# The opening loads of a hybrid attention, Fourier and Hyena layer: x, the first adaLN block and the first weights ahead of the filter constants

## The chip, the cores and the metric

The kernel runs on one core of one Trainium2 chip. The metric is device microseconds of one execution, the median of several runs. Every time below is counted from the start of the profiled execution's span unless it is called a duration.

## The reference

One layer of a diffusion backbone over 384 tokens (128 of context, 256 latent, in a grid 64 wide) of width 2048. Everything is float32.

```python
def _modulated_proj(x, cvec, norm_g, w_ada, b_ada, w_in):
    ada = jax.nn.silu(cvec) @ w_ada + b_ada
    shift, scale, gate = jnp.split(ada, 3, axis=-1)
    h = _rmsnorm(x, norm_g) * (1.0 + scale[:, None, :]) + shift[:, None, :]
    return h @ w_in, gate
...
    proj, gate = _modulated_proj(y, c_ctx[None, :], norm_g[l], w_ada[l], b_ada[l], w_in[l])
    q, k, v = _qkv(proj, q_norm_g[l], k_norm_g[l])
    att = _context_attention(q, k, v)
    kf = _hyena_filter_fft(len_prompt, f_w1[l], f_b1[l], f_freq[l], f_w2[l], f_b2[l], f_w3[l])
    y = _branches_residual(y, proj, gate, att, conv_w[l], conv_b[l], kf, hy_bias[l], w_br[l], w_out[l])
```

The Hyena filters come from a small network of two sine layers over positions and a last matrix f_w3, times a decaying window. They are normalised by the sum of their absolute values and taken to the frequency domain:

```python
    h = jnp.sin(f_freq * (z @ f_w1 + f_b1))
    h = jnp.sin(f_freq * (h @ f_w2 + f_b2))
    h = (h @ f_w3).astype(jnp.float32).reshape(L, HYENA_ORDER, 2, HY_W)
    h = h * jnp.exp(-t[:, :, None, None] * deltas)
    h = h / (jnp.sum(jnp.abs(h), axis=0, keepdims=True) + EPS)
    ...
    return jnp.fft.rfft(k2, axis=0)
```

## The kernel before

**Main work.** Weights stream from HBM in tiles of 256 rows by 512 columns (512 KB, tile w). ScalarE rounds each to a high part wh, VectorE takes the rest as a low part wl, and TensorE forms three products (high by high, low by high, high by low). The first stage of the main flow is hc_part: four column blocks of the Hyena input, taken in groups of rows (GROUPS). Group 0 needs the modulated activations h of the first 256 channels, group 1 those of the next 256, groups 2 to 4 of 512 more each. A group has 4 or 8 weight tiles, and a tile is 24 matmuls 384 columns wide.

**The adaLN blocks.** h exists only when the adaLN maps of its channels are done. ADA lists five blocks: first column, width, and at which main step (a main step is half a weight tile) their loads begin and how densely they follow. Blocks 0 and 1 are 256 channels wide (4 MB of w_ada each), blocks 2 to 4 are 512 wide (8 MB each). Block 0 has 8 loads, each a tile of 512 KB issued as two transfers of 256 KB, through N_ADA = 4 buffers. From block 1 on a step takes two loads. When a block's sums are complete, ada copies them to a row (ada_row), transposes it, forms scale and shift (am, sm) and modulates xT into h_hi and h_lo. The event h0 is block 0 done.

**Other opening work.** x_norm takes x in six tiles of 512 KB: a square with a row sum, transposes into xT, and at the end the reciprocal norm rstd_b. filters computes the sine layers f1 and f2, splits f_w3 on GpSimd (split_w3: a cast and a subtraction for each half), then forms 12 filter products of two matmuls 512 columns wide, each multiplied by the window win on VectorE into hw, and later sums of absolute values (habs), reciprocals, row broadcasts and the transforms specE, specO, specC. Those transforms are needed by hyena, which waits for hc, filters and all adaLN blocks.

**Order.** The class Weave decides the program order of TensorE and of the SP queue by a planned time: each flow (filters, ada_flow, x_norm, hyena, ada_gate, main, with a priority number, low first) yields steps with a planned TensorE time, a latency, events to wait for, and for loads the planned DMA time and the number of buffers. LOAD is the planned time of a 512 KB transfer, PAIR that of a weight tile on TensorE, X_AT the planned arrivals of x. Up to h0 the order of ScalarE, VectorE and GpSimd is the program's as well; after it a scheduler sets theirs. SP issues in order: a load whose buffer is not free holds up all loads behind it.

The loads before stand in this order. SP issues mlp (inputs of the sine layers), six tiles of x, win, then block 0 with the waits of its four buffers, and in between, after the fifth load, the first 512 columns of blob (Fourier matrices). GpSimd issues fw3 (f_w3) in two transfers, ScalarE's queue issues first (small vectors and the identity). The first weight tile is loaded when block 0 is through.

Of the kernel before, what the change touches and what calls it, by code (L numbers as in the profile page):

```python
# [18 lines left out]
P = 128  # L19
# [83 lines left out]

ADA = ((0, 256, -KT, 0), (256, 256, 0.1, 0.5), (512, 512, 4, 0.7), (1024, 512, 14, 1), (1536, 512, 30, 1))
GROUPS = ((0, (0,)), (1, (1,)), (2, (2, 3)), (3, (4, 5)), (4, (6, 7)))

BLOB = (("fwde", 256), ("fwdo", 256), ("inve", 256), ("invo", 256), ("fnetl", 516), ("fnetc", 130), ("chan", 256))
# [20 lines left out]
class Weave:  # L130
# [7 lines left out]

    def __init__(self):
        self.t = 0.0  # L140
        self.dma = 16.7
        self.flows = []
        self.events = {}
        self.slots = {}
        self.steps = 0
# [59 lines left out]
MM3 = 0.65  # L205
MM2 = 0.44
TR = 0.11
LOAD = 1.6
X_AT = (6.9, 8.4, 9.8, 12.7, 14.2, 15.6)
PAIR = 3.92  # L210


@with_exitstack
def hybrid_block(ctx: ExitStack, tc: tile.TileContext, a: dict):
# [25 lines left out]
    def s6(shape, dt, name):  # L240
        return big.tile(shape, dt, tag="s6", name=name, bufs=N_BIG)
# [24 lines left out]

    first = const.tile([P, 139 + P], F32, name="first")
    mlp = s6([64, TOK + 192], F32, "mlp")
    nc.sync.dma_start(out=mlp, in_=a["mlp"])
    nc.scalar.dma_start(out=first, in_=a["first"])  # L270
    vec, ident = first[:, 0:139], first[:, 139:139 + P]
    zfeat, fw1, fw2 = mlp[0:33, 0:TOK], mlp[0:33, TOK:TOK + 64], mlp[0:64, TOK + 64:TOK + 192]
    nmat = sum(w for _, w in BLOB)
    blob = hyc.tile([P, nmat], F32, name="blob")
    fw3 = [s6([P, 1024], F32, "fw3") for _ in range(2)]
    for q in range(2):
        nc.gpsimd.dma_start(out=fw3[q], in_=a["f_w3"][:, 1024 * q:1024 * q + 1024])
    win = s6([P, NT, HW], F32, "win")
    mats = {}
    c0 = 0  # L280
    for n, w in BLOB:
# [80 lines left out]
    def x_norm():  # L362

        ss = work.tile([P, 2, NT], F32, tag="ss", name="x_ss", bufs=1)
        arrival = iter(X_AT)
        for t in range(NT):
            for q in range(2):
                yield step(8 * TR, at=next(arrival))
                xt = xps[t, q]
                junk = s6([P, 1024], F32, "xjunk")  # L370
                nc.scalar.activation(junk, xt, AF.Square, accum_out=ss[:, q, t:t + 1])
                for g2 in range(2):
                    pt = acc()
                    for k in range(4):
                        c0 = 512 * g2 + P * k
                        nc.tensor.transpose(out=pt[:, P * k:P * k + P], in_=xt[:, c0:c0 + P], identity=ident)  # L376
                    (nc.scalar.copy, nc.vector.tensor_copy)[g2](out=xT[2 * q + g2][:, :, P * t:P * t + P],
                                                                in_=pt.rearrange("p (k c) -> p k c", k=4))
        s1 = work.tile([P, NT], F32, tag="ss1", name="x_s1", bufs=1)
        r1 = work.tile([P, NT], F32, tag="ss2", name="x_r1", bufs=1)  # L380
        yield step(0.0, lat=2.3)
        nc.vector.tensor_tensor(out=s1, in0=ss[:, 0], in1=ss[:, 1], op=ALU.add)
        yield step(0.0, lat=0.2)
        yield from rsqrt(r1, s1, NT, 1.0 / D)
        yield step(0.7, lat=0.3)
        pt = acc()
        for t in range(NT):
            mm(pt[:, P * t:P * t + P], r1[:, t:t + 1].broadcast_to([P, P]), ident)
        nc.scalar.copy(out=rstd_b, in_=pt[:, 0:TOK])
        W.signal("x")  # L390
# [6 lines left out]
    def ada(b, c0, wd, pace, rate):  # L397
# [2 lines left out]
        pa = None  # L400

        def load(i):
            w = adap.tile([P, nk, 2, wd], F32, tag="ada", name="w_ada", bufs=N_ADA)
            rows = w_ada[P * nk * i:P * nk * i + P * nk, 0:2 * D].rearrange("(k p) (t c) -> p k t c", p=P, t=2)
            for k in range(nk):
                nc.sync.dma_start(out=w[:, k], in_=rows[:, k, :, c0:c0 + wd])
            return w

        n = 1 if b == 0 else 2
        for i in range(0, KT // nk, n):  # L410
            yield step(0.48 * n, dma=n * LOAD, tag="ada", bufs=N_ADA // n, pace=pace + rate * nk * i)
            ws = [load(i + k) for k in range(n)]
            pa = pa or acc()
            for k in range(n * nk):
                kt = nk * i + k
                for j in range(4):
                    mm(pa[32 * j:32 * j + 32, 0:hw], cond[:, kt, :],
                       ws[k // nk][:, k % nk, j // 2, hw * (j % 2):hw * (j % 2) + hw], kt == 0, kt == KT - 1)
            if b == 0 and i == 4:
                nc.sync.dma_start(out=blob[:, 0:N_FWD], in_=a["blob"][:, 0:N_FWD])  # L420
                split(blob[:, 0:N_FWD].rearrange("p (q c) -> p q c", q=4), fwd_hi, fwd_lo)
        if b == 0:
            ahead.append(weights(w_in, 0, OFF_HC))
            next(ahead[0])
        yield step(nh * TR, lat=0.6, after=("x",), wait=1.0)
        with tc.high_priority():
# [37 lines left out]

    ahead = []

    def weights(src, kp, c0):

        w = stage.tile([P, 2, 512], F32, tag="w", name="w", bufs=N_W)
        nc.sync.dma_start(out=w, in_=src[256 * kp:256 * kp + 256, c0:c0 + 512].rearrange("(k p) c -> p k c", p=P))  # L470
        wh = stage.tile([P, 2, 512], F32R, tag="hi", name="wh", bufs=N_HI)
        wl = stage.tile([P, 2, 512], F32R, tag="lo", name="wl", bufs=N_LO)
        nc.scalar.copy(out=wh, in_=w)  # L473
        yield
        nc.vector.tensor_tensor(out=wl, in0=w, in1=wh.bitcast(F32), op=ALU.subtract)  # L475
        yield wh, wl

    def products(src, c0, kps, n, product, evac, done=lambda kp: (), final=False):


        ps = None
        for kp in kps:
            last = kp == kps[-1]
            rounds = (((0, 0), (1, 0), (0, 1)),) if last and final else (((0, 0), (1, 0)), ((0, 1),))
            for r, parts in enumerate(rounds):
                pe = 2 * len(parts) * PAIR / (6 * n)
                for j in range(n):
                    if (r, j) == (0, 0):
                        yield step(pe, dma=LOAD, tag="w", bufs=N_W, prep=2.3, count=2 * pe / PAIR, after=done(kp),
                                   wait=2.0)  # L490
                        with tc.high_priority():
                            *_, w = ahead.pop() if ahead else weights(src, kp, c0)
                        ps = ps or [acc() for _ in range(n)]
                    else:
                        yield step(pe, tag="w", bufs=N_W, count=2 * pe / PAIR)
                    for k in range(2):
                        for px, pw in parts:
                            product(ps[j], j, 2 * kp + k, px, w[pw][:, k, :], kp == kps[0] and k == px == pw == 0,
                                    last and k == pw == 1)
                    if last and (r, j) >= (len(rounds) - 1, 0):  # L500
                        with tc.high_priority():
                            evac(j, ps[j])
# [34 lines left out]
    def filters():  # L537
# [15 lines left out]
        f2 = yield from sin_layer(p2, P, 10, "f2")  # L553
        f2s = split(f2, tmp("f2h", None, F32R)[:, 0:TOK], tmp("f2l", None, F32R)[:, 0:TOK])
        fw3s.append(split_w3(fw3[1]))
        hw = [s6([P, NT, HW], F32, f"hw{j}") for j in range(4)]
        for jj, t in ((0, 0), (0, 1), (0, 2), (2, 0), (2, 1), (2, 2)):
            for j in (jj, jj + 1):
                yield step(MM2, lat=0.3, at=17.2)
                ph = aux()  # L560
                ts_, cs_ = slice(P * t, P * t + P), slice(512 * (j % 2), 512 * (j % 2) + 512)
                for i, f in enumerate(f2s):
                    mm(ph, f[:, ts_], fw3s[j // 2][:, cs_], i == 0, i == 1)
                nc.vector.tensor_tensor(out=hw[j][:, t, :], in0=ph, in1=win[:, t, :], op=ALU.mult)
        for s, ts in ((CONTEXT, (0,)), (LATENT, (1, 2))):
            pz = aux()
            for t in ts:
                yield step(0.0, lat=1.0)
                ab = [tmp("habs") for _ in range(4)]
                for j in range(4):  # L570
                    nc.scalar.activation(ab[j], hw[j][:, t, :], AF.Abs)
                yield step(1.0, lat=2.2, after=("h0",), wait=4.0)
                for j in range(4):
                    mm(pz[32 * j:32 * j + 32, :], ones, ab[j], t == ts[0], t == ts[-1])
            r = tmp("hrec")
# [293 lines left out]
    def ada_flow():  # L869
        for b, (c0, wd, pace, rate) in enumerate(ADA):  # L870
            yield from ada(b, c0, wd, pace, rate)
            if b == 2:
                late_constants()
        close_pool()
        W.signal("ada")

# [162 lines left out]
            yield from tok_block(w_out, 512 * ob, m, ev_out, final=(ob == 3), done=done)  # L1039

    x_loads()
    nc.sync.dma_start(out=win, in_=a["win"])
    E = mybir.EngineType
    with tc.manual_schedule(engines={E.PE, E.SP}):
        with tc.manual_schedule(engines={E.Activation, E.DVE, E.Pool}):
# [36 lines left out]
```

## Time and profile before

| | us |
|---|---|
| median of 3 runs | 1313.8 |
| lowest and highest | 1312.83, 1315.71 |
| profiled execution, time | 1315.51 |
| profiled execution, span | 1313.7 |
| TensorE busy in the span | 1281.3 |
| VectorE, ScalarE, GpSimd busy | 716.1, 461.7, 186.3 |

TensorE carries a matmul for 98% of the span, at a mean granted clock of 0.992. Durations below are those of the profiled execution, which is 1.7 us over the median; a change in time is worked out on it and carried over to the median.

### The profile page before, as it was taken

Reading aid. Unit: us, or ns where it says so; the run is one execution under the profiler, and the core shown is the slowest. Engines: PE = TensorE matmul, PEld = TensorE weight load, DVE = VectorE, ACT = ScalarE, POOL = GpSimd, SP = SyncE. Lnnn points to the kernel's source line nnn. Section 1 sums busy time; section 2 is a strip of 40 time slices with the busy share of each in tenths; the row PEclk is TensorE's granted clock in tenths of the full one; section 3 lists DMA queues with packets and bytes.
Section 4 is the critical chain, followed back from the end, with each engine's and each line's share of the span. In section 5 each row is a group of like instructions: output and inputs, shape, how many; then the busy total and the mean of one; then the engine's idle time right before and its main releaser. Section 6 shows DMA issues by size and latency. Waiting matters only on the chain.

```text
span 1313.7 us, 16781 instructions
## 1 busy us (share of the span) xinstructions
PE 1281.3 (98%) x6554; PEld 1072.6 (82%) x6554; DVE 716.1 (55%) x1077; ACT 461.7 (35%) x722; POOL 186.3 (14%) x201
## 2 busy tenths in 40 slices
PE   7899999999999999999999999999999999999997
PEld 4667879878888988889888888888888888888886
DVE  6566638878454225552344776565647652354442
ACT  4424324421344245432544333323333333242221
POOL 2046300135010002210110110011001100110000
PEclk9889999999999999999999999999999999999999
DMA  8788774322374545554443665554665544464551
GB/s 284 246 297 288 261 264 131 111 81 82 100 160 130 144 133 111 131 120 136 106 120 84 202 191 176 169 178 145 191 189 167 178 140 129 142 195 135 158 151 65
DMA packets 111183, 210.94 MB, mean 161 GB/s; under 512 B 8192, under 2 KB 16768, under 8 KB 111104
## 3 DMA queue, kind: packets, MB, share of 16 engines
q1 hardware_dynamic: 107200, 198.98, 49.2%
q0 software_dynamic: 3760, 10.76, 4.9%
q8 instruction: 51, 0.84, 0.3%
q14 instruction: 28, 0.23, 0.1%
q10 hardware_dynamic: 144, 0.14, 0.0%
HBM read 205.65 MB, written 4.19 MB: 160 GB/s over the span
## 4 chain that ended last, share of the span: by engine, by line
PE 94%; DMA 3%; DVE 1%; ACT 1%; POOL 1%; issue 0%; SPq 0%; ACTq 0%
PE acc L253 86%; PE aux L253 6%; DMA w<-in_w_in 1%; DMA w_ada<-in_w_ada 1%; DMA x<-in_x_prompt 1%; PE aux L851 0%; PE aux L783 0%; PE aux L996 0%; POOL yim L678 0%; DVE wl L475 0%; PE acc L376 0%; ACT wh L473 0%; PE aux L663 0%; POOL yre L678 0%; DVE f_n L529 0%
## 5 line engine op out<-in xcount | busy, mean ns | idle before, releaser
L475 DVE TENSOR_TENSOR wl<-w,wh 128x1024 fp32r<-128x1024 f32 x272 | 343.1, 1262 | 413.1 <-PE acc L253 304.2
L473 ACT CAST wh<-w 128x1024 fp32r<-128x1024 f32 x272 | 286.4, 1053 | 679.0 <-PE acc L253 586.3
L253 PE MATMUL acc<-wh,h_hi 128*128 128x512 f32 x912 | 361.0, 396 | 0.6 <-ACT gateA L743 0.6
L253 PE MATMUL acc<-wh,h_lo 128*128 128x512 f32 x912 | 356.1, 390 | 0.0
L253 PE MATMUL acc<-wl,h_hi 128*128 128x512 f32 x912 | 239.9, 395 | 0.0
L253 PEld LDWEIGHTS acc<-wh,h_hi 128*128 128x128 f32 x912 | 171.3, 188 | 36.4 <-ACT gateA L743 1.1
L253 PEld LDWEIGHTS acc<-wh,h_lo 128*128 128x128 f32 x912 | 171.5, 188 | 35.0 <-issue 0.7
L253 PEld LDWEIGHTS acc<-wl,h_hi 128*128 128x128 f32 x912 | 168.6, 188 | 34.4 <-issue 1.4
L253 PE MATMUL acc<-h_hi,wh 128*128 128x384 f32 x448 | 155.2, 347 | 5.7 <-DVE hc L634 2.0
L253 PE MATMUL acc<-h_lo,wh 128*128 128x384 f32 x448 | 151.6, 338 | 0.0
L931 DVE SCALAR_TENSOR_TENSOR gate_part<-w_gate,cond,gate_part 128x512 f32<-128x512 f32 x120 | 90.1, 796 | 43.4 <-DMA w_gate<-in_w_ada 43.3
L253 PEld LDWEIGHTS acc<-h_hi,wh 128*128 128x128 f32 x448 | 85.1, 190 | 16.6 <-issue 7.8
L253 PE MATMUL acc<-h_hi,wl 128*128 128x384 f32 x448 | 90.2, 339 | 0.0
L253 PEld LDWEIGHTS acc<-h_lo,wh 128*128 128x128 f32 x448 | 85.1, 190 | 2.2 <-issue 0.7
L1018 POOL TENSOR_TENSOR merged<-merged,mt 128x512 f32<-128x512 f32 x21 | 34.8, 1679 | 361.7 <-DVE mt L1017 361.7
L253 PEld LDWEIGHTS acc<-h_hi,wl 128*128 128x128 f32 x448 | 78.4, 188 | 3.4 <-issue 2.7
L253 PE MATMUL acc<-wh,m_hi 128*128 128x512 f32 x192 | 75.0, 390 | 0.0
L253 PE MATMUL acc<-wh,m_lo 128*128 128x512 f32 x192 | 74.8, 390 | 0.0
L253 PE MATMUL acc<-wl,m_hi 128*128 128x512 f32 x192 | 49.9, 390 | 0.0
L253 PEld LDWEIGHTS acc<-wh,m_hi 128*128 128x128 f32 x192 | 36.0, 188 | 7.4
L253 PEld LDWEIGHTS acc<-wh,m_lo 128*128 128x128 f32 x192 | 36.1, 188 | 7.4
L253 PEld LDWEIGHTS acc<-wl,m_hi 128*128 128x128 f32 x192 | 35.9, 188 | 7.3
(257 smaller groups left out, 1301.1 us busy)
## 6 DMA issues: line engine op xcount, KB each, us to landing
w<-in_w_in SPq DMA_DIRECT2D x208, 512.0 KB, 3.7
w_ada<-in_w_ada SPq DMA_DIRECT2D x48, 512.0 KB, 5.3
w<-in_w_br SPq DMA_DIRECT2D x32, 512.0 KB, 4.2
w_gate<-in_w_ada SPq DMA_DIRECT2D x64, 256.0 KB, 4.1
w<-in_w_out SPq DMA_DIRECT2D x32, 512.0 KB, 4.1
w_ada<-in_w_ada SPq DMA_DIRECT2D x32, 256.0 KB, 5.8
x<-in_x_sample SPq DMA_DIRECT2D x4, 512.0 KB, 12.3
bm<-in_rpb POOLq DMA_DIRECT2D x32, 64.0 KB, 6.0
```

Source lines behind the costliest of these rows:

```text
L253: nc.tensor.matmul(out, lhsT, rhs, start=start, stop=stop)
L473: nc.scalar.copy(out=wh, in_=w)
L475: nc.vector.tensor_tensor(out=wl, in0=w, in1=wh.bitcast(F32), op=ALU.subtract)
L931: nc.vector.scalar_tensor_tensor(out=part[s], in0=w, scalar=cond[:, kt, s:s + 1], in1=before, op0=ALU.mult, op1=ALU.add)
L1018: (nc.vector if ob == 3 and bi == 2 else nc.gpsimd).tensor_tensor(out=m32[:, t, :], in0=m32[:, t, :], in1=x, op=ALU.add)
```

## The change

The opening loads get another order, and the filter products another place:

- SP starts with x. mlp moves to ScalarE's queue, behind first.
- Block 0 is loaded at once behind x: all eight loads are issued before any of its matmuls. Loads 4 to 7 get buffers of their own (from the pool s6) in place of a wait on the first four. The first weight tile w0 is loaded just ahead of block 0's last load.
- fw3 moves from GpSimd's queue to SP, behind block 0. win and the blob columns move to SP behind the first main steps (pace 2.2).
- The 12 filter products wait for h0 and 7 planned us more; the blob split follows them. The planned wait for h0 that stood ahead of the habs sums goes.
- xjunk is one tile in place of six allocations.
- Planner constants: LOAD 1.6 to 1.42, PAIR 3.92 to 4.15, earlier X_AT, block 2's loads at 0.6 in place of 0.7 steps, blocks 3 and 4 from step 13 and 27 in place of 14 and 30.

```diff
-ADA = ((0, 256, -KT, 0), (256, 256, 0.1, 0.5), (512, 512, 4, 0.7), (1024, 512, 14, 1), (1536, 512, 30, 1))
+ADA = ((0, 256, -KT, 0), (256, 256, 0.1, 0.5), (512, 512, 4, 0.6), (1024, 512, 13, 1), (1536, 512, 27, 1))
...
-        self.dma = 16.7
+        self.dma = 10.5
...
-LOAD = 1.6
-X_AT = (6.9, 8.4, 9.8, 12.7, 14.2, 15.6)
-PAIR = 3.92
+LOAD = 1.42
+X_AT = (5.0, 6.3, 7.6, 8.9, 10.2, 11.5)
+PAIR = 4.15
...
-    nc.sync.dma_start(out=mlp, in_=a["mlp"])
     nc.scalar.dma_start(out=first, in_=a["first"])
+    nc.scalar.dma_start(out=mlp, in_=a["mlp"])
...
-    for q in range(2):
-        nc.gpsimd.dma_start(out=fw3[q], in_=a["f_w3"][:, 1024 * q:1024 * q + 1024])
     win = s6([P, NT, HW], F32, "win")
+
+    def filter_constants(*which):
+        for n in which:
+            if n < 2:
+                nc.sync.dma_start(out=fw3[n], in_=a["f_w3"][:, 1024 * n:1024 * n + 1024])
+            elif n == 2:
+                nc.sync.dma_start(out=win, in_=a["win"])
+            else:
+                nc.sync.dma_start(out=blob[:, 0:N_FWD], in_=a["blob"][:, 0:N_FWD])
...
+        junk = s6([P, 1024], F32, "xjunk")
...
-                junk = s6([P, 1024], F32, "xjunk")
...
-            w = adap.tile([P, nk, 2, wd], F32, tag="ada", name="w_ada", bufs=N_ADA)
+            if b == 0 and i >= N_ADA:
+                w = s6([P, nk, 2, wd], F32, "w_ada")
+            else:
+                w = adap.tile([P, nk, 2, wd], F32, tag="ada", name="w_ada", bufs=N_ADA)
...
+        ready = []
+        if b == 0:
+            for i in range(KT // nk):
+                if i == KT // nk - 1:
+                    w0 = weight_load(w_in, 0, OFF_HC)
+                ready.append(load(i))
+            filter_constants(0, 1)
         for i in range(0, KT // nk, n):
-            yield step(0.48 * n, dma=n * LOAD, tag="ada", bufs=N_ADA // n, pace=pace + rate * nk * i)
-            ws = [load(i + k) for k in range(n)]
+            yield step(0.56 * n, dma=n * LOAD, tag="ada", bufs=N_ADA // n, pace=pace + rate * nk * i)
+            ws = [ready[i]] if ready else [load(i + k) for k in range(n)]
...
-            if b == 0 and i == 4:
-                nc.sync.dma_start(out=blob[:, 0:N_FWD], in_=a["blob"][:, 0:N_FWD])
-                split(blob[:, 0:N_FWD].rearrange("p (q c) -> p q c", q=4), fwd_hi, fwd_lo)
         if b == 0:
-            ahead.append(weights(w_in, 0, OFF_HC))
+            W.dma += 3 * LOAD
+            ahead.append(weights(w_in, 0, OFF_HC, w0))
...
         fw3s.append(split_w3(fw3[1]))
+        yield step(0.0, pace=2.2)
+        filter_constants(2, 3)
+        W.dma += 2 * LOAD
...
-                yield step(MM2, lat=0.3, at=17.2)
+                yield step(MM2, lat=0.3, after=("h0",), wait=7.0)
...
+        split(blob[:, 0:N_FWD].rearrange("p (q c) -> p q c", q=4), fwd_hi, fwd_lo)
...
-                yield step(1.0, lat=2.2, after=("h0",), wait=4.0)
+                yield step(1.0, lat=2.2)
...
     x_loads()
-    nc.sync.dma_start(out=win, in_=a["win"])
```

weight_load is the allocation and load of a weight tile, taken out of weights without other change; products takes w0 as the first tile and plans no load for it.

## Rows read from the trace of the kernel before

**Rows 1.** The page: busy time of each engine, share of the span, instructions.
```profile
PE 1281.3 (98%) x6554; PEld 1072.6 (82%) x6554; DVE 716.1 (55%) x1077; ACT 461.7 (35%) x722; POOL 186.3 (14%) x201
```

**Rows 2.** Stretches: length, each engine's busy time (instructions), granted clock, DMA share, GB/s.
```profile
8.00:18.00 10.00, 7.63 (x30) 6.18 (x31) 4.83 (x6) 5.52 (x10) 6.82 (x4) 1.00 1.03 411
...
23.50:27.00 3.50, 3.50 (x41) 2.00 (x41) 3.43 (x11) 1.25 (x3) 0.00 (x0) 1.00 0.27 77
...
52.00:66.00 14.00, 14.00 (x143) 11.41 (x141) 6.16 (x16) 7.60 (x17) 1.03 (x2) 1.00 0.57 174
66.00:76.00 10.00, 7.47 (x63) 4.82 (x64) 6.92 (x13) 5.14 (x11) 0.00 (x0) 1.00 1.00 353
```

**Rows 3.** Timeline of the SP queue up to 26 us: start, duration, issue.
```profile
1.37 1.04 SPq L357 DMA_DIRECT2D x<-in_x_prompt  x2
...
12.53 0.37 SPq L406 DMA_DIRECT2D w_ada<-in_w_ada  x1
...
17.64 0.37 SPq L406 DMA_DIRECT2D w_ada<-in_w_ada  x1
...
25.42 0.88 SPq L406 DMA_DIRECT2D w_ada<-in_w_ada  x2
```

**Rows 4.** GpSimd's DMA queue, 4.5 to 8 us: packets, MB, share of 16 engines.
```profile
q0 software_dynamic: 119, 0.45, 47.6%
```

**Rows 5.** Timeline of TensorE, 22 to 40.9 us: start, duration, instruction [idle before].
```profile
22.39 0.39 PE L253 MATMUL aux<-fw3hl,f2h 128*128 128x512 f32 x1
22.62 0.40 PE L253 MATMUL aux<-fw3hl,f2l 128*128 128x512 f32 x1
...
24.72 0.64 PE L253 MATMUL acc<-w_ada,cond 128*32 128x128 f32 x16
...
33.31 0.42 PE L253 MATMUL acc<-w_ada,cond 128*32 128x128 f32 x8 [0.25 <-DMA w_ada<-in_w_ada]
34.01 0.42 PE L253 MATMUL acc<-w_ada,cond 128*32 128x128 f32 x8 [0.27 <-DMA w_ada<-in_w_ada]
...
36.70 0.65 PE L253 MATMUL acc<-w_ada,cond 128*32 128x128 f32 x8 [0.71 <-DMA w_ada<-in_w_ada]
...
40.17 0.69 PE L253 MATMUL acc<-h_hi,wh 128*128 128x384 f32 x1 [1.93 <-ACT h_hi L453]
```

**Rows 6.** TensorE's granted clock in stretches of 1 us: busy, clock, DMA share, GB/s.
```profile
44.00:45.00 1.00, 1.00 (x28) 0.50 0.90 317
...
78.00:79.00 1.00, 1.00 (x13) 0.50 1.03 393
```

**Rows 7.** Timeline of TensorE at the end of group 0, 73 to 76 us.
```profile
73.05 0.64 PE L253 MATMUL acc<-w_ada,cond 128*32 128x256 f32 x8 [0.71 <-DMA w_ada<-in_w_ada]
75.50 0.45 PE L253 MATMUL acc<-h_hi,wh 128*128 128x384 f32 x1 [1.81 <-ACT wh L473]
```

**Rows 8.** Timeline of the SP queue at the end of group 0.
```profile
50.83 15.66 SPq L406 DMA_DIRECT2D w_ada<-in_w_ada  x10
66.61 0.39 SPq L470 DMA_DIRECT2D w<-in_w_in  x1
```

**Rows 9.** VectorE's filter products and ScalarE's last filter copies by source line.
```profile
L564 DVE TENSOR_TENSOR hw<-aux,win x12: 680/682/692, 22.7 to 32.0; 128x512 f32<-128x512 f32 x12
...
L611 ACT COPY specC<-aux x2: 578/584/589, 125.6 to 170.3; 128x512 f32<-128x512 f32 x2
```

**Rows 10.** Timeline of TensorE: the transposes of block 4's rows.
```profile
198.19 0.44 PE L431 MATMUL aux<-first,ada_row 128*128 128x128 f32 x2 [0.70 <-DVE ada_row L428]
```

**Rows 11.** Timeline of VectorE and GpSimd, 14 to 41 us.
```profile
14.70 0.36 DVE L528 TENSOR_SCALAR f_n<-f_a 128x384 f32<-128x384 f32 x1
14.87 2.40 POOL L547 TENSOR_TENSOR fw3hl<-fw,fw3hl 64x1024 fp32r<-64x1024 f32 x1
15.10 2.40 DVE L529 TENSOR_SCALAR f_n<-f_n 128x384 f32<-128x384 f32 x1
...
38.74 1.40 DVE L452 SCALAR_TENSOR_TENSOR xT<-xT,am,rstd_b 128x256 f32<-128x256 f32 x4
```

## What the change is predicted to do

> **What bounds the kernel now.** First the page: TensorE carries a matmul for 1281.3 us [rows 1], so only about 32 us of the span can be won without taking work from it. What counts as busy at the opening is partly filler, so the opening is read next, stage by stage. The DMA engines are full at 411 GB/s from 8 to 18 us, then move 77 GB/s from 23.5 to 27 [rows 2]. The SP queue says why: its loads of block 0 need buffers that TensorE has to free, and after the early ones no pair goes out until 25.42 [rows 3]. TensorE reaches the first block-0 matmuls only at 24.72, behind transposes and filter products [rows 5]. From there on block 0 arrives late: its matmuls wait on loads that land 0.70 us apart (33.31, 34.01), the last starts at 36.70, and the first main matmul at 40.17 [rows 5]. The chain through the opening is therefore loads, not TensorE. After 40.17 it is mostly TensorE, with one hole: from 52 to 66 us the DMA engines are at 0.57, from 66 to 76 at 1.00, and TensorE loses 2.53 us there [rows 2] (10.00 less 7.47), most of it for a weight tile whose issue at 66.61 stood behind ten w_ada transfers [rows 7, 8]. The granted clock is 0.50 (1.2 GHz) from 44 to 45 us, still in the fifth us of main work, and again from 78 to 79, behind the hole [rows 6].
>
> **The first loads.** The last tile of x lands at 17.64: that issue was released by it, and the five tiles behind the second land from 12.53 on, 1.28 us apart (17.64 less 12.53, over 4) [rows 3]. Two things leave the front of x. GpSimd's queue moved fw3, taking 47.6% of the engines between 4.5 and 8 us [rows 4]; its 1.05 MB at 411 GB/s [rows 2] are 2.55 us. SP's own start with x moves from 1.37 [rows 3] to the place of mlp, some 0.6 us. mlp is still loaded and I book nothing for its move to ScalarE's queue. So x is complete at 17.64 - 2.55 - 0.6 = 14.5. Behind it come 16 transfers of block 0 at 0.70 us [rows 5] and w0, twice the bytes, at 1.4: 12.6 us, hence 27.1 for the last one. Before, that matmul started at 36.70. **Gain: 9.6 us.** Bounds: with 353 GB/s [rows 2], 0.74 us for 262 KB, it is 9.6 - 18 x 0.04 = 8.9, and without the 0.6 it is 8.3; with 411 GB/s, 0.64 us, it is 10.7.
>
> The own buffers are what makes this possible: SP now issues all of block 0 without a wait on TensorE, and what is queued behind them (fw3, then block 1) inherits no stall. x_norm hides under it: rstd_b needs x at 14.5, six squares and copies on ScalarE, and a short chain on VectorE that no longer has 12 multiplications of 0.68 us in between [rows 9]; 12 us of loads cover it. With that cover gone it would delay h0 one for one. The single xjunk costs nothing, since its writers are all on ScalarE, in order.
>
> The way from the last block-0 matmul to the first main one, 3.47 us (36.70 to 40.17) [rows 5], has the same instructions. The clock at the start of the main work I take as before: at 0.50 for the first 5 us.
>
> **The filter products.** They are 12 times two matmuls, 0.23 us apart (22.39, 22.62) [rows 5]: 24 x 0.23 = 5.5 us. Before they ran while block 0 was awaited; now they stand in the main stage, where TensorE is the bound. **Cost: 5.5 us.** Lower bound 0, if they fall into holes that TensorE has anyway; upper bound 8.2, if VectorE's 12 multiplications at 0.68 [rows 9] paced them. I take 5.5, because the new order puts them between the quarters of the second and third weight tile, some 1.1 us apart, which VectorE can follow. win must land before the fourth can go on; it is two load steps behind w0 and fw3 in the queue, and lands, at these rates, about when the second tile begins.
>
> **The constants behind.** fw3, win and blob, together 2.1 MB, are 5.7 us at 0.70 us per 262 KB that move past h0. Group 0 has the room: fw3, block 1, three weight tiles, win and blob are 7.9 MB, 21 us at that rate, from 27.1 on, to 48; TensorE has four tiles of 4.15 by PAIR, the products and the slow clock (5 us at half speed, 2.5 lost), 24.6 us from 30.6 on, to 55. So it costs nothing there while that cover lasts, else up to 5.7. The filters' end moves later by the same order; their last copies are at 170.3 [rows 9], and hyena also waits for block 4, whose rows come at 198.19 [rows 10]: 28 us of cover.
>
> **GpSimd's splits.** A subtraction of split_w3 takes 2.40 us, and a VectorE instruction that began in it took 2.40 where its like took 0.36 [rows 11]: the two exclude each other. Before, that fell beside the loads of x. Now fw3 lands at about 28.4, and the subtraction after the cast can meet the modulation that makes h0: by the offsets of [rows 5, 11] the four steps of 1.40 us begin at 38.74 - 9.6 = 29.1. **Cost: 0 to 2 x 2.4 = 4.8; I take 1.2**, half of one, as the two instructions needed first may slip ahead. The Trainium skill (GPSIMD Engine Reference, Specifications) says that GpSimd shares its SBUF interfaces with VectorE, in contention with two-port modes and two-input instructions. It speaks against this change, and the trace agrees by that 2.40. By the rule at its worst the sum below would lose nearly all its gain; by the row's half it keeps it.
>
> **The end of group 0.** Following the new constants step by step, one adaLN group more and four row broadcasts come to stand between the fourth and fifth weight tile. They fill the hole that is 0.71 + 1.81 now [rows 7], and the tile's load is queued behind fewer bytes at a time. I take 2.0 us of gain. Bounds: all of 2.5 and the slow clock after it, some 3 us, so 5.5; or a loss of 6, see below. PAIR nearer to what tiles take changes the order further on; I book 0, and 2 us either way for the range.
>
> **Sum:** -9.6 + 5.5 + 1.2 - 2.0 = -4.9. On the profiled execution (1315.5, of which 1313.7 are the span) that gives 1310.6; on the median 1313.8 it gives 1308.9. Differences under 0.2%, 2.6 us, are not told from no change here.
>
> **Rivals.**
> - **The hole closes entirely**, with the slow clock behind it: -9.6 + 5.5 + 1.2 - 5.5 = -8.4, and with the loads at their better bound -9.5: 1304 to 1305. For it: half of the engines' time stands idle just before the hole [rows 2]. Against: block 2's loads are packed denser, 0.6 for 0.7.
> - **The hole grows** (slower than before). The fifth weight tile is issued only after the adaLN groups ahead of it have found buffers; with eight transfers ahead, 2.1 MB at 353 GB/s [rows 2], it waits 5.9 us, and the clock falls after it, 3 us. -9.6 + 5.5 + 1.2 + 5.9 + 3 = +6: 1320. It decides as soon as the hole is 3 us longer than now, for then nothing is left. For it: the same 2.1 MB more stand ahead of block 2 relative to the main work. Against: the main work, too, has 5.5 us more to do meanwhile.
> - **GpSimd holds up h0**: both subtractions meet VectorE's needed steps, 4.8 in place of 1.2: -1.3, 1312.5, no measurable change. For it: the times computed above overlap. Against: the second comes 3.4 us after the first, when h0 should be made.
> - **The loads are no sooner**: the DMA engines are full before as after, so block 0 gains only the idle stretch 23.5 to 27, 3.5 x (1 - 0.27) = 2.6 us. Then -2.6 + 5.5 + 1.2 - 2.0 = +2.1: 1316. Against: 2.1 MB really leave its front.
>
> **How the numbers follow.** Chances: the forecast 0.46, the hole closed 0.20, the hole grown 0.13, GpSimd 0.14, loads no sooner 0.07. The likeliest gives 1309, with 1305 to 1313 as its own range from the bounds of loads and products. The range 1301 to 1317 takes in all but the hole grown in full and a little beyond the best. Faster: 0.40 of the forecast, all of the hole closed, a little of GpSimd: 0.62. Same: 0.06 of the forecast, most of GpSimd, some of the last: 0.22. Slower: the hole grown and some of the last: 0.16.
>
> **What would show it.** x complete near 14.5 with landings about 1.28 us apart; block 0's last matmul near 27 and the first main one near 31; no stretch of idle DMA before 40 us; the products between the quarters of tiles two and three, with no wait on win above 1 us; VectorE steps of 2.4 us near 30 if GpSimd interferes; TensorE idle near the fifth tile at most 1 us. The prediction is wrong if main starts later than 33, if that hole is longer than 5 us, or if idle time appears after 200 us, where I expect none.

## The result and the profile after

The changed kernel takes 1321.28 us (median of 4, 1319.04 to 1323.11); the kernel before, beside it, 1313.42 (median of 4). The ratio is 1.0056, 95% interval [1.0036, 1.0076]: 7.9 us slower, where 1309 was forecast, and outside the range. The profiled execution is the quickest of the four: 1319.04, its span 1317.3, 3.6 us over the span of before.

TensorE is busy for nearly the time of before, now 1276.7 of a longer span. One line of the page, to set beside [rows 1]:

```profile
PE 1276.7 (97%) x6554; PEld 1072.5 (81%) x6554; DVE 721.6 (55%) x1077; ACT 462.7 (35%) x722; POOL 185.2 (14%) x199
```

So the loss is idle time, and the opening is read first. TensorE's timeline from 22 us, to set beside [rows 5] (last column: idle before, and its releaser):

```profile
23.84 1.65 PE L253 MATMUL acc<-first,x_r 128*128 128x128 f32 x6 [3.96 <-DVE x_r L350]
25.42 3.23 PE L253 MATMUL acc<-w_ada,cond 128*32 128x128 f32 x80
...
36.25 0.69 PE L253 MATMUL acc<-h_hi,wh 128*128 128x384 f32 x1 [6.84 <-ACT h_hi L469]
37.13 0.69 PE L253 MATMUL acc<-h_lo,wh 128*128 128x384 f32 x1 [0.19 <-DVE h_lo L471]
```

The loads came out as forecast, but by two errors that cancel. The last x tile, issued by 3.84, landed at 12.94, 1.6 us sooner than the 14.5 forecast. From there to block 0's last load (27.23, 27.1 forecast) it took 14.3 us and not 12.6: block 0's transfers landed 0.75 us apart in place of 0.70, and w0 took 2.27 in place of 1.4. Block 0's last 80 matmuls run in one piece without a wait on a load and end at 28.65, 8.7 us before the end of 37.35 in [rows 5]. They stand on TensorE behind the broadcast of the reciprocal norm, which waits 3.96 us for x_r (23.84); so the chain of x_norm was not hidden by the loads to its end. But the first main matmul starts at 36.25, only 3.9 us before its 40.17. The way between the two is 7.60 us in place of 2.82, and TensorE idles 6.84 us of it for h_hi. The prediction had itself called a start after 33 its failure. What stands in that gap is on three other engines. GpSimd from 20 us:

```profile
28.57 1.04 POOL L569 CAST fw3hl<-fw 128x1024 fp32r<-128x1024 f32 x1 [27.25 <-DMA fw<-in_f_w]
29.69 2.34 POOL L570 TENSOR_TENSOR fw3hl<-fw,fw3hl 64x1024 fp32r<-64x1024 f32 x1
32.09 1.04 POOL L569 CAST fw3hl<-fw 128x1024 fp32r<-128x1024 f32 x1
33.21 2.40 POOL L570 TENSOR_TENSOR fw3hl<-fw,fw3hl 64x1024 fp32r<-64x1024 f32 x1
```

VectorE and ScalarE in the same stretch:

```profile
29.59 0.22 DVE L457 TENSOR_TENSOR sm<-aux,first 128x2 f32<-128x2 f32 x2
29.72 2.39 DVE L459 TENSOR_TENSOR am<-am,first 128x2 f32<-128x2 f32 x2
32.17 4.25 DVE L468 SCALAR_TENSOR_TENSOR xT<-xT,am,rstd_b 128x256 f32<-128x256 f32 x4
```
```profile
25.91 1.05 ACT L493 CAST wh<-w 128x1024 fp32r<-128x1024 f32 x1
34.21 1.05 ACT L493 CAST wh<-w 128x1024 fp32r<-128x1024 f32 x1 [7.26 <-DMA w<-in_w_in]
35.17 1.83 ACT L469 ACTIVATE h_hi<-xT,sm 128x256 fp32r<-128x256 f32 x4
```

Two things meet. Two am steps, each two elements wide, take 2.39 us together where their like take 0.22, and four xT steps 4.25 where they take 1.40 [rows 11]: 5.0 us together. The am steps end with the first subtraction (32.11 and 32.03), the xT steps run through the second (33.21 to 35.61). And ScalarE holds, ahead of h_hi, the cast of the *second* weight tile, which waits 7.26 us for its load. Before, only the first tile's cast stood there. SP shows why that load is late: it is issued at 26.51, behind fw3 and the first four transfers of block 1.

```profile
20.49 1.09 SPq L281 DMA_DIRECT2D fw<-in_f_w  x2
22.06 4.06 SPq L417 DMA_DIRECT2D w_ada<-in_w_ada  x4
26.51 0.37 SPq L485 DMA_DIRECT2D w<-in_w_in  x1
```

Further on, TensorE is busy throughout the products (the first two of 24, which run from here to 59.6):

```profile
46.79 0.39 PE L253 MATMUL aux<-fw3hl,f2h 128*128 128x512 f32 x1
47.02 0.39 PE L253 MATMUL aux<-fw3hl,f2l 128*128 128x512 f32 x1
```

One starts 0.23 us behind the other: 24 x 0.23 = 5.5 us, as forecast (from start to next start, all 24 take 5.7). The hole at the end of group 0 is still there, now as three waits on block 2's loads in place of [rows 7], and later waits on other engines follow:

```profile
71.06 0.64 PE L253 MATMUL acc<-w_ada,cond 128*32 128x256 f32 x8 [0.69 <-DMA w_ada<-in_w_ada]
73.10 0.64 PE L253 MATMUL acc<-w_ada,cond 128*32 128x256 f32 x8 [0.40 <-DMA w_ada<-in_w_ada]
75.36 1.08 PE L253 MATMUL acc<-w_ada,cond 128*32 128x256 f32 x8 [1.62 <-DMA w_ada<-in_w_ada]
...
104.27 0.41 PE L253 MATMUL acc<-h_hi,wh 128*128 128x384 f32 x1 [1.16 <-DVE hc L661]
```

The stretches, to set beside [rows 2] (length; busy time and count of TensorE, weight load, VectorE, ScalarE, GpSimd; granted clock, DMA share, GB/s):

```profile
23.50:27.00 3.50, 3.16 (x38) 2.83 (x42) 0.25 (x2) 1.43 (x2) 0.00 (x0) 0.54 1.06 384
40.00:42.00 2.00, 2.00 (x11) 2.00 (x10) 0.01 (x1) 0.00 (x0) 0.00 (x0) 0.79 0.06 14
52.00:66.00 14.00, 14.00 (x140) 11.02 (x139) 9.41 (x23) 6.13 (x13) 0.00 (x0) 1.00 0.54 166
66.00:76.00 10.00, 7.08 (x64) 3.49 (x62) 6.12 (x10) 4.50 (x10) 0.00 (x0) 0.95 0.98 334
```

The early DMA idleness is gone (384 GB/s from 23.5 to 27, 77 before), but a new one stands at 40 to 42 us (14 GB/s, before 376), and the hole from 66 to 76 is 2.92 us, before 2.53. The load of the fifth weight tile is issued later than the 66.61 of [rows 8], behind twelve transfers of block 2 in place of ten:

```profile
45.93 23.27 SPq L417 DMA_DIRECT2D w_ada<-in_w_ada  x12
69.33 0.39 SPq L485 DMA_DIRECT2D w<-in_w_in  x1
```

### The profile page after: what moved, and what is told of

Same layout as the page of the kernel before. It is cut to its first block, busy times and chain, and to the rows that moved or that the text cites. A ratio compares the mean times of both kernels' runs of the same rounds, so it can differ in the third digit from the quotient of the medians.

```text
span 1317.3 us, 16793 instructions
## 1 busy us (share of the span) xinstructions
PE 1276.7 (97%) x6554; PEld 1072.5 (81%) x6554; DVE 721.6 (55%) x1077; ACT 462.7 (35%) x722; POOL 185.2 (14%) x199
## 4 chain that ended last, share of the span: by engine, by line
PE 90%; issue 3%; DMA 2%; DVE 2%; ACT 1%; POOL 1%; SPq 0%; ACTq 0%; POOLq 0%
PE acc L253 83%; PE aux L253 5%; DMA w<-in_w_in 1%; DMA mlp<-in_mlp 1%; DMA w_ada<-in_w_ada 0%; PE aux L810 0%; PE aux L1024 0%; DVE wl L495 0%; PE aux L878 0%; DVE xT L468 0%; POOL yim L705 0%; ACT wh L493 0%; DVE cm L704 0%; ACT xjunk L379 0%; PE acc L384 0%
## 5 line engine op out<-in xcount | busy, mean ns | idle before, releaser
L253 PE MATMUL acc<-h_hi,wl 128*128 128x384 f32 x448 | 93.5, 341 | 0.0
```

The source lines that it names most:

```text
L253: nc.tensor.matmul(out, lhsT, rhs, start=start, stop=stop)
```

## The experiments

Twelve kernels ran, each beside the kernel before. For the early stretch a mark is used below: the start of VectorE's rounding rest wl of the 25th weight tile, at 202.22 us before and 204.99 after, so +2.8. From there to the last tile the differences of the runs move by 0.9 to 2.5 us more. A mark is that of one execution, and the profiled executions lie between 2.2 us under their kernel's median (the changed kernel) and 2.9 over it (the second tile ahead); so a difference of marks of 3 us or less, without a wait that accounts for it, does not rank two kernels. The medians do.

**Splits out of the way.** In the changed kernel a one-column GpSimd copy of h_lo stands ahead of the splits:

```diff
+            guard = const.tile([P, 1], F32, name="guard")
+            nc.gpsimd.tensor_copy(out=guard, in_=hl[0][:, 1, 0:1].bitcast(F32))
+            fw3s.extend(split_w3(fw3[q]) for q in range(2))
```

> The changed kernel with GpSimd's two splits of fw3 held back until h0 is made: a one-column copy of the last part of h_lo stands ahead of them on GpSimd. Loads, and the order on TensorE, VectorE, ScalarE and SP, are those of the changed kernel. Theory (the two subtractions cost VectorE's modulation 5.0 us): the steps on the way to h0 take 0.22 and 1.40 us again, the first main matmul comes near 31.5 in place of 36.25, the products do not wait (their operand is split by 41), and the time is 4 to 5 us under the changed kernel, so 2 to 4 us over the kernel before. Rival (the head start is lost again before 200 us, since the loads of block 1 and the weight tiles, not TensorE, then set the pace): main starts as early, but the 25th weight tile comes less than 2 us earlier than in the changed kernel. Second rival (GpSimd's splits now meet the first low parts of the weights): the low parts of tiles one and two take 2.4 us more, and half of the gain goes.

Measured 1318.91, ratio 1.0039 [1.0021, 1.0058]. VectorE's chain is short again, but the first main matmul comes at 36.20 and not near 31.5, because ScalarE waits as before:

```profile
29.51 0.22 DVE L466 TENSOR_TENSOR am<-am,first 128x2 f32<-128x2 f32 x2
29.78 1.41 DVE L475 SCALAR_TENSOR_TENSOR xT<-xT,am,rstd_b 128x256 f32<-128x256 f32 x4
```
```profile
34.41 1.04 ACT L503 CAST wh<-w 128x1024 fp32r<-128x1024 f32 x1 [7.40 <-DMA w<-in_w_in]
35.36 1.49 ACT L476 ACTIVATE h_hi<-xT,sm 128x256 fp32r<-128x256 f32 x4
```

The splits do stretch VectorE; alone they do not decide.

**Second tile's load ahead of fw3,** splits as changed:

```diff
+            loaded.append(weight_load(w_in, 0, OFF_HC + 512))
             filter_constants(0, 1)
```

> The changed kernel with one load moved: the second weight tile is loaded right behind block 0, ahead of fw3; the GpSimd splits stay where the change put them. Theory (two blockers in a row, VectorE held up by the GpSimd splits and ScalarE held up by the cast of the second weight tile, which waits for its load): that cast now runs near 29 us without a wait, fw3 lands some 1.4 us later, VectorE is still held up by the splits, so the first main matmul comes between 33.5 and 36.5 in place of 36.25, and the time is 0 to 2.5 us under the changed kernel, 1318.5 to 1321. Rival (the splits alone hold h0): the first main matmul at 36 to 38, 1320 to 1323. Rival (the second tile's cast alone): first main matmul near 31.5, 1316 to 1317.

Measured 1321.23, ratio 1.0058 [1.0042, 1.0074], no faster than the changed kernel. The cast now runs at 28.93. A first matmul slips in at 31.95, but then TensorE waits 5.30 us and goes on at 37.94: the rival (the splits alone hold h0) was right on time and place.

```profile
31.95 0.69 PE L253 MATMUL acc<-h_hi,wh 128*128 128x384 f32 x1 [2.60 <-ACT h_hi L470]
37.94 0.69 PE L253 MATMUL acc<-h_lo,wh 128*128 128x384 f32 x1 [5.30 <-DVE h_lo L472]
```
```profile
29.93 5.13 DVE L469 SCALAR_TENSOR_TENSOR xT<-xT,am,rstd_b 128x256 f32<-128x256 f32 x4
34.99 3.55 DVE L472 SCALAR_TENSOR_TENSOR h_lo<-xT,sm,h_hi 128x256 fp32r<-128x256 f32 x4
```

**Both together,** the two edits above:

> The changed kernel with both suspects removed: the second weight tile is loaded right behind block 0, ahead of fw3, and the GpSimd splits wait until h0's activations are made. Theory: h_hi starts near 30.5, the first main matmul comes at 31 to 32 in place of 36.25, and 4.5 to 5 us of it reach the end: 1316 to 1317, 1 to 3 us over the kernel before. Rival (a third cause stands behind the two): the first main matmul after 33.5. Rival (the early start is lost again in group 0 because block 1 or the later tiles are not there yet): main starts at 31 to 32 but the time stays at 1319 to 1321.

Measured 1315.11, ratio 1.0012 [0.9996, 1.0027]: 2.1 us over before, not told from no change, and 6.2 under the changed kernel. Main starts at 31.45, as the theory said, with ScalarE and VectorE without a stretched step:

```profile
28.54 1.04 ACT L504 CAST wh<-w 128x1024 fp32r<-128x1024 f32 x1 [1.80 <-DMA w<-in_w_in]
30.60 1.49 ACT L477 ACTIVATE h_hi<-xT,sm 128x256 fp32r<-128x256 f32 x4 [1.02 <-DVE xT L476]
```
```profile
31.45 0.69 PE L253 MATMUL acc<-h_hi,wh 128*128 128x384 f32 x1 [1.97 <-ACT h_hi L477]
```

So there were two blockers, either of which held h0 until 36. But of the 8.7 us by which main starts earlier than before, 5.5 go to the products, and the other 3.2 are gone at the 25th tile, which stands at +0.4. From the first main matmul to the mark TensorE idles 8.24 us, before 6.72; the longest waits are 1.52 us on w_ada at 71.25 and 2.06 on ada_row at 146.56. So 1.5 us are added idle time; the rest is matmuls that start further apart, some of them at a granted clock of 0.50 from 148 to 150 us, right behind the second wait. That rest was not taken apart.

**fw3 behind the first main steps.** filter_constants(0, 1) and both splits move behind `yield step(0.0, pace=2.2)`:

> The changed kernel, with the loads of fw3, and so GpSimd's two splits of it, moved from behind block 0 to behind the first main steps, ahead of win; nothing else. Theory (GpSimd's subtractions hold up VectorE's modulation that makes h0): in the changed kernel the steps L459 and L468 took 2.39 and 4.25 us where the kernel before has 0.22 and 1.40, 5.0 us together, so here they take 0.2 and 1.4 again, the first main matmul comes at 31 to 32 in place of 36.25, and the time falls by about 4.5 us against the changed kernel, to the level of the kernel before or 1 us under it. Rival (the way to h0 is slow for another reason, such as full DMA engines or the later x): first main matmul stays near 36, time within 1 us of the changed kernel. Second rival (the head start is won, but the weight and block-1 loads now 1 MB further back or the holes behind take it again): main starts near 31, time falls by less than 2 us.

Measured 1327.00, ratio 1.0098 [1.0077, 1.0119]: slower, though main starts 2.8 us earlier than in the changed kernel. The mark is at +10.2. VectorE shows where it went: reciprocals of the filter sums, which now come due beside block 1, stand ahead of its ada_row, and TensorE idles 5.84 us at 65.84.

```profile
60.83 3.39 DVE L603 RECIPROCAL hrec<-hrec 128x128 f32<-128x128 f32 x4
...
65.50 0.28 DVE L443 COPY ada_row<-acc 128x128 f32<-128x128 f32 x1
```

**The same, reciprocals behind h1** (`yield step(0.0, after=("h1",))` ahead of hrec):

> The kernel of e1_fw3_late (1327.0) with one planned wait more: the reciprocals of the filter sums wait for h1, the second adaLN block. Theory (in e1_fw3_late the head start of 2.8 us was lost where VectorE had four reciprocals, 3.4 us, and what they wait for ahead of block 1's row, so that TensorE idled 5.84 us before it, with a slow clock after): the idle time before block 1's row falls under 1.5 us, and the time by 6 to 10 us, to 1317 to 1321. Rival (the loss lay in fw3 and its splits coming late for the products): no change from 1327.

Measured 1315.95, ratio 1.0008 [0.9992, 1.0024], the mark at +1.5: 11 us better by that one wait. That settles where the run before it lost its time.

**fw3 early, as before the change,** on GpSimd's queue ahead of everything, the rest as changed:

> The changed kernel with fw3 loaded from GpSimd's queue at the start again, as in the kernel before; nothing else. Theory (GpSimd's subtractions are the loss): the splits fall at 10 to 18 us beside x, where they can slow the sine layer's VectorE steps but not h0; block 0 lands 2.5 us later, since 1 MB shares the engines with x again; the first main matmul comes at 33 to 34.5; time 2 to 3 us under the changed kernel, so 3 to 5 us over the kernel before. Rival (the two kernels differ by the position of fw3 on the DMA engines alone): main starts 2.5 us later than in the changed kernel, near 38.5, and the time rises by 2.5.

Measured 1320.17, ratio 1.0043 [1.0029, 1.0056]. VectorE's am and xT steps are 0.22 and 1.41 us again, yet main starts at 37.34, between theory and rival. fw3's bytes explain part: x is complete at 15.82, 2.9 us later than in the changed kernel. But rstd_b is copied at 30.68, 5.2 us later (25.53), because the splits, now at 10.42 to 17.70, hold the VectorE steps of the first sine layer instead:

```profile
11.78 2.41 DVE L553 TENSOR_SCALAR f_n<-f_n 64x384 f32<-64x384 f32 x1
14.23 3.88 DVE L555 SCALAR_TENSOR_TENSOR f_a<-f_n,f_a 64x384 f32<-64x384 f32 x2
```

In the changed kernel these take 0.35 and 1.14 us. TensorE waits 4.14 us for f_a, and the last transposes of x, block 0 and the norm's broadcast stand behind it. These 4.8 us beside x are as much as the splits cost beside h0 (5.0).

**Splits out of the way, and mlp first on SP,** to ask whether its landing at 8.34 us (3.62 before) matters:

> The kernel of e5_splits_wait_h0 with mlp at the head of SP's queue again in place of second on ScalarE's. Theory (in the changed kernel mlp landed at 8.4 us where it had landed at 3.7, because ScalarE's two loads share the engines with x; the sine layers and the transposes of x wait for it on TensorE, and rstd_b stands ahead of block 0's last five loads until 25.4): rstd_b comes 1 to 3 us earlier, x itself 0.4 later, h0 0.5 to 1 us earlier than in e5_splits_wait_h0, the time 0 to 1 us under it. Rival (block 0's loads alone set h0): no difference or 0.4 us more.

Measured 1320.28, ratio 1.0046 [1.0029, 1.0063]. mlp is used at 3.62, and rstd_b is copied at 22.68, 2.6 us earlier than in the run with the splits moved (25.31). But x is complete at 14.07 and block 0's last load lands at 28.90 (13.01 and 27.43 there), and the second tile's cast, held by its load until 35.90, still stands ahead of h_hi: main starts at 37.69. Nothing is gained while the loads and that cast set h0.

**The products alone moved,** on the kernel before:

```diff
-                yield step(MM2, lat=0.3, at=17.2)
+                yield step(MM2, lat=0.3, after=("h0",), wait=7.0)
...
-                yield step(1.0, lat=2.2, after=("h0",), wait=4.0)
+                yield step(1.0, lat=2.2)
```

> The kernel before with one part of the change alone: the 12 filter products, and their planned wait, behind h0. Theory (a product is TensorE time that was free before h0 and is paid in full behind it, 24 matmuls at 0.23 us): 5.5 us more behind h0, less what block 0 gains since its matmuls no longer stand behind five products, at most 2.7 us: slower than the kernel before by 3 to 5.5 us. Rival (they fill holes that TensorE has in the main stage anyway): same as the kernel before, or up to 2.6 us faster.

Measured 1339.28, ratio 1.0192 [1.0170, 1.0214]: far beyond both expectations. Block 0's matmuls end no sooner (38.45, before 37.35), and TensorE idles 9.35 us ahead of block 1's row at 77.10; on VectorE the four reciprocals (72.08, 3.39 us) stand ahead of ada_row (76.76). It is the jam of the run with fw3 late, found here in another kernel. The mark is at +21.6: beside the 9.35 and the products' 5.5 there is another wait of 4.70 at 122.10 (on VectorE's scaling of hw); the rest was not followed.

**The planner's constants alone,** on the kernel before (ADA, LOAD, PAIR):

> The kernel before with the planner's constants of the changed kernel alone: LOAD, PAIR, and the paces and starts of blocks 2 to 4. Theory (the constants only shift which instructions stand next to each other, and explain the rest of the loss: 1.2 us of holes before 200 us and 0.9 behind): slower than the kernel before by 1 to 3 us. Rival (they are what lengthened the hole at the end of group 0, and the rest is chance): slower by 3 us or more. Second rival: no difference.

Measured 1315.67, ratio 1.0009 [0.9997, 1.0022]: no difference told. The mark is at -2.9, the last tile at -1.9, but the profiled execution (1313.61) is the quickest of the twelve, so this is no gain. From the mark to the last tile 1.0 us is given back, and as much in the whole change (+2.8 to +3.7). This part comes with the constants: behind 205 us TensorE idles 5.35 us here and 5.30 in the changed kernel, before 4.61, and both have a wait of 0.7 us for ScalarE's pT (at 663.12 and 668.72) that the kernel before lacks. The constants also put the twelve transfers of block 2 ahead of the fifth weight tile, whose load is issued at 70.04 here.

**Block 0's loads alone,** own buffers and all issued at once, on the kernel before:

> The kernel before with the loads of block 0 alone changed: all eight issued at once behind x and win, four of them into buffers of their own, the first weight tile ahead of the last. fw3 stays at the start on GpSimd's queue, win behind x, the filter products stay before h0, and the constants are those of before. Theory (the loads are worth what the waits on buffers cost, and the loss lies in the products' move): x complete at 17.6 as before, win 1.9 us more, 12.6 us of loads: the last block-0 matmul at 32 in place of 36.7, the first main one at 35.5 to 36.5, the time 3 to 5 us under the kernel before. Rival (block 0's matmuls stand behind transposes, products and rstd_b on TensorE, so earlier loads help little): main starts at 38 or later, time within 2.6 us of the kernel before.

Measured 1315.02, ratio 1.0013 [0.9999, 1.0027]. Main starts at 40.58. What was won on the loads is held on ScalarE by what stands ahead of h_hi: blob's cast and the habs behind it, then both weight tiles' casts.

```profile
34.48 0.62 ACT L301 CAST fwd_hi<-blob 128x512 fp32r<-128x512 f32 x1 [1.76 <-DMA blob<-in_blob]
35.00 2.19 ACT L584 ACTIVATE habs<-hw 128x512 f32<-128x512 f32 x4
37.10 1.03 ACT L486 CAST wh<-w 128x1024 fp32r<-128x1024 f32 x1
38.78 1.04 ACT L486 CAST wh<-w 128x1024 fp32r<-128x1024 f32 x1 [0.66 <-DMA w<-in_w_in]
39.73 1.49 ACT L462 ACTIVATE h_hi<-xT,sm 128x256 fp32r<-128x256 f32 x4
```

**The same with the second tile's load behind block 0 and blob ahead of it** (blob is loaded behind win, and the broadcast of the norm gets a planned time of 27 us; the three edits were not told apart):

> The kernel before with block 0's loads all issued at once (buffers of their own), the first and the second weight tile and blob around them, the filter products left where they were. Theory (in this version what held h0 was ScalarE's queue, with casts of blob and of the second weight tile that waited for loads ahead of h_hi): the first main matmul at 38 to 39 in place of 40.17, 1 to 2 us under the kernel before, 1312 to 1313.5. Rival (fw3 and win ahead of x and the products on TensorE hold block 0 itself, so nothing is won): first main matmul at 40 or later, 1314 to 1316.

Measured 1312.77, ratio 0.9993 [0.9980, 1.0006]. Main starts at 37.93 and the mark is at -2.4, as the theory said; -0.7 is left at the last tile, and the time is not told from that of before.

**The products in the hole,** on the version with both blockers gone (`after=("h1",)` for the products):

> As the version with both suspects removed, and the filter products wait for block 1 (h1) in place of h0 and 7 planned us, so that they come where TensorE waits between group 0 and group 1 and not into its busy stretch. Theory (the products cost 5.5 us because TensorE was busy where they stood): 2 to 3 us less than the version with both suspects removed, 1312 to 1315. Rival (VectorE's reciprocals, which follow the products, come ahead of the next adaLN row and hold it up, or the filters are late for the Hyena stage): the same or up to 10 us more, 1316 to 1326.

Measured 1321.09, ratio 1.0052 [1.0037, 1.0067]: the rival. From 60 to 80 us TensorE now loses 0.85 us in place of 3.09, but 1.61 at 46.98 and 1.71 at 84.54 come in, and the filters are late, and their GpSimd steps (casts, additions and subtractions; the first and the last of five in a row are shown) meet the modulation that makes an h_lo:

```profile
150.41 0.60 POOL L629 CAST evod<-ev 128x512 fp32r<-128x512 f32 x1
...
154.03 1.28 POOL L626 TENSOR_TENSOR ev<-hw,hw 128x512 f32<-128x512 f32 x1
```
```profile
148.71 8.84 DVE L479 SCALAR_TENSOR_TENSOR h_lo<-xT,sm,h_hi 128x128 fp32r<-128x128 f32 x7
157.47 0.83 DVE L636 COPY specO<-specO 128x512 f32<-128x512 f32 x1
```
```profile
160.84 1.06 PE L253 MATMUL aux<-evod,fwd_hi 128*32 128x512 f32 x2 [5.06 <-ACT specO L644]
```

One of those seven h_lo steps, begun at 150.02, took 5.43 us and ended at 155.46, with the last of the five (155.30); the median of its 32 is 0.48. The copy of specO behind it was late, and TensorE idled 5.06 us.

## Why the prediction was wrong

On the profiled pair the forecast -4.9 became +3.6.

| term | predicted | measured |
|---|---|---|
| end of block 0's matmuls | -9.6 | -8.7 (37.35 to 28.65) |
| from there to the first main matmul | +1.2 | +4.8 (2.82 to 7.60) |
| products | +5.5 | +5.5 |
| holes up to the 25th tile, the clock with them | -2.0 | +1.2 (see below) |
| afterwards | 0 | +0.9 (+2.8 to +3.7) |
| sum | -4.9 | +3.7 |

The holes' term is what is left: from the first main matmul to the mark the kernels take 162.05 and 168.74 us, with the same 1161 matmuls but for the 24 products; 6.69 - 5.5 = 1.2. TensorE's idle time in that stretch goes from 6.72 to 8.51. This term and the next come from one execution of each kernel and are smaller than the spread between executions.

- **The loads** and **the products** came out right, the products by their mechanism. The loads' gain is within 0.9 us partly by luck: x was forecast 1.6 us too late and the loads behind it 1.7 too quick, which cancels. x at the head of SP's queue was worth more than the 0.6 booked: with fw3 back on GpSimd's queue x is still complete at 15.82, before at 17.63. (Two slips entered no term: the landings 1.28 us apart are those of tiles two to six, five tiles from the second on, and fw3, win and blob at 0.70 are 5.6 us, not 5.7.) The 0.9 is the cover that was booked as whole: with the norm 2.6 us earlier (mlp first on SP) the last matmul of block 0 ends 0.47 us behind its load (28.90 to 29.37), in the changed kernel 1.4 (27.23 to 28.65).
- **The step that failed** is "The way from the last block-0 matmul to the first main one, 3.47 us (36.70 to 40.17) [rows 5], has the same instructions." It did not: a cast that waits for the second weight tile had come into ScalarE's program order ahead of h_hi. I had followed TensorE's and SP's order through the new constants, not ScalarE's. The run with the splits moved starts main at 36.20, the run with the tile moved stops behind one matmul and goes on at 37.94; only both gone gives 31.45. Every run that issues block 0's loads at once has it there, with the old constants too (block 0's loads alone), and the two runs without that edit (the products alone, the constants alone) have not. Which line of the edit brings it was not tried.
- **GpSimd's splits** were seen as a mechanism and mis-sized: 1.2 booked, 4.8 as the upper bound, 5.0 measured (2.39 less 0.22 and 4.25 less 1.40), part of it beside a cast, which was not counted at all. The reason I gave for a quarter, that needed steps slip ahead, has no row behind it; the am step was caught at its start. The Trainium skill (GPSIMD Engine Reference, Specifications) says that the shared interfaces contend with VectorE instructions of two SBUF inputs; am and xT are such, and the trace agrees by those 5.0 us. By that rule at its worst the sum lost its gain, and that was the better reading.
- **The hole** was forecast to shrink by 2.0. It did not; 66 to 76 us lost 2.92 in place of 2.53. The reason given failed: the fifth tile's load was to be queued behind fewer bytes, and it stands behind twelve transfers in place of ten, issued at 69.33 in place of 66.61; and the adaLN groups that were to fill the hole wait there for their own loads (0.69, 0.40 and 1.62 us). Waits of 1.16 and 2.00 us came at 104.27 and 150.34, while 1.71 and 0.70 before the mark (196.55 and 198.19) went. With both blockers gone the remaining gain is lost between the first main matmul and the mark too. So the forecast could not have come true by an undisturbed h0 alone: that version measured +2.1, not -4.9.
- **Afterwards** 0 was booked and idle time behind 200 us called a sign of being wrong: behind 205 us it went from 4.61 to 5.30, and the constants bring it.
- **No rival** was right as priced. "GpSimd holds up h0" named one cause, but kept the hole's gain.

The median difference, 7.9 us, is 4.3 more than that of the profiles: the profile of before lies 2.1 over its median, that of after 2.2 under. The changed kernel's executions order by their mean granted clock: 1319.04 at 0.994, 1321.12 and 1321.44 at 0.991, 1323.11 at 0.988. In the profiled one TensorE is at 0.50 (1.2 GHz) from 34 us, in the idle time ahead of main, to the 41st, and again from 75 to the 79th; the profiled execution of before is at 0.50 longer at that place, from 77 to the 84th, which favours the change in the profiled pair. The version with only the second tile moved was profiled at 0.988; its clock is low from 31 to the 42nd and from 75 to the 83rd microsecond. First after, then that version:

```profile
40.00:41.00 1.00, 1.00 (x5) 1.00 (x4) 0.01 (x1) 0.00 (x0) 0.00 (x0) 0.57 0.11 29
78.00:79.00 1.00, 1.00 (x6) 0.82 (x5) 0.84 (x2) 0.25 (x1) 0.52 (x1) 0.80 1.07 389
```
```profile
41.00:42.00 1.00, 1.00 (x7) 1.00 (x7) 0.00 (x0) 0.00 (x0) 0.00 (x0) 0.87 0.08 16
82.00:83.00 1.00, 1.00 (x7) 1.00 (x6) 0.35 (x1) 0.00 (x0) 0.00 (x0) 0.89 0.42 160
```

That longer slow stretches make the rest of the difference in the changed kernel itself is argued from this; its other executions have no trace.

## What to carry to other kernels

When loads are moved forward, follow every engine's in-order queue from the last load to the first use, and ask of each instruction ahead of the critical one what it waits for: one cast for the *next* tile can undo more than half of the gain (4.8 of 8.7 us here). Work that filled a wait costs its full length where it lands next (5.5 us here), and what feeds or follows it (splits, reciprocals) lands beside other critical steps, where it cost as much again (5.0, 5.84 and 9.35 us). Of two blockers in parallel, removing either leaves the first use where it was; remove both before you drop a theory.

## What was not expected of the hardware

- A waiting VectorE step is not always freed by the end of one GpSimd instruction: the h_lo step of 5.43 us sat through two casts and three two-input steps, one behind the other, and ended only where the next one started 0.08 us after the last (155.30 to 155.38). In the changed kernel the am steps came through in the 0.06 us between the first subtraction and the second cast (32.03 to 32.09). And a cast alone holds such a step too: the first xT step of the changed kernel, beside the cast from 32.09 to 33.13, took 1.24 us (32.17 to 33.41), where the first of the four took 0.48 in the kernel before.
- mlp, on ScalarE's queue behind first and beside x on SP's, landed 7.15 us after its issue (1.19 to 8.34); before, ahead of x on SP's own queue, 2.88 (0.74 to 3.62).
